# One encoder layer on one core: the last forgetting pair by squares and DRAM, two differential norms by squares

## The chip, the cores and the metric

The kernel runs on one core of a Trainium2 chip. The metric is the device time of one execution in microseconds. The core has a matrix engine (TensorE, "PE" in the profile, its weight loads "PEld"), three engines for elementwise work (VectorE "DVE", ScalarE "ACT", GpSimd "POOL"), and SyncE ("SP"), which here only issues transfers. Each engine works off its own list of instructions in the order in which they were built, and waits on semaphores for the others.

## The reference

The reference is one layer of a streaming encoder on 512 tokens of 1024 channels, all in float32. The first sub-layer has four token mixers that read one normed input, among them differential attention (4 heads, two score maps each) and forgetting attention (8 heads, frame-causal):

```python
# differential attention, per head
a = p[:, :, 0] - lam * p[:, :, 1]
ya = _rms_norm(a @ v, diff_norm) * (1.0 - lambda_init)     # norm over the head's 128 channels
# forgetting attention, per head (64 channels)
s = q @ k.T * scale + c_q[:, None] - c_k[None, :]          # c: cumulative sum of log-forget
yf = softmax(where(causal, s, -inf)) @ v
# merge
mixed = sum over n of sigmoid(h @ w_gate + b_gate)[n] * (branch[n] @ w_branch[n]), @ w_out
```

Cross-attention to 256 memory tokens and a gated MLP with a short convolution follow.

## The kernel before

**Arithmetic.** Every product is made of matmuls in a reduced float32 format on operands that are split into a high and a low part: `mm3` (L250) issues high by high, high by low and low by high. So each weight tile that comes from DRAM is cast by ScalarE (L198, "wh") and subtracted by VectorE (L199, "wl"), and each activation is split in the same way (`split`, L158).

**Jobs and background.** `run_blocks` (L212) takes jobs from a generator. A job is a weight tile of 128 x 1024 and a body of matmuls on it; weights are fetched three jobs ahead, into two raw tiles and four split ones. Beside the jobs there is a background (L47): the attention tasks are generators that yield a cost and a least distance to the next step, and are advanced between jobs. `bg.drain(name)` runs the named tasks to their end. The order in which the instructions of each engine then stand is set by the tile framework's scheduler, from its own timeline; `tc.issue_after` ties one instruction behind another.

**Order of the jobs** (`mixer_jobs`, L1202). After the convolution and the short convolution come the differential heads with the convolution branch's gates, then the values of the forgetting heads, then the projections of query and key of the four forgetting pairs, two heads each (`kv_blocks`), with jobs of the first branch's gates (`gate_blocks(0, "a")`, 12 jobs in all: two gates and a branch, four times) dealt out behind the pairs 1, 2 and 3 (L1238). Behind them the forgetting tasks are drained, and `last_branch_jobs` (L1347) begins the branch that reads the forgetting heads.

**A forgetting pair** (`f_task`, L1059). In each of the steps 0 to 3 one block of 128 queries is scored for both heads (`scores`), VectorE adds mask and bias and takes the row minimum (L1129), ScalarE takes the exponential (L1135), and both scale by the reciprocal (L1140, L1142). The probabilities lie with queries on partitions; the value products need keys there. For the pairs 0, 1 and 2 (`far`) VectorE transposes 32 x 32 squares (`turn_squares`, L854), SP stores the result to DRAM (`put`, L859) and loads it back with the squares in their places (`get`, L866), and `split_in_place` casts (L872) and subtracts (L873). For the pair 3 `to_keys_major` (L836) transposes blocks of 128 x 128 on TensorE (L247) into the PSUM bank "tr" and splits from there. The value products follow in two halves (`values`, L883) into two "av" banks, one a head, and are evacuated at the end (L1153, L1154), then split into `y["f"]`.

**A differential head** (`a_task`, L901). The heads 0 to 2 go the same way by DRAM, head 3 by TensorE. At the end each head is normed: four transposes on TensorE bring tokens onto partitions, ScalarE squares (L958), VectorE reduces (L960), GpSimd takes the power, VectorE scales (L962), and four transposes bring channels back, into a split (L970). The convolution's norm (`conv_norm_task`, L700) does without them: it transposes squares, reduces over 32 channels, and sums the four partial sums with one product by a tiled identity (`over_channels`, L877).

**Banks.** PSUM has eight banks: two each of "sc", "mm" and "av", one each of "tr0" and "tr1". Jobs take turns among tags (`bank()`, L97): "mm" and "tr0" from the heads on, "mm" alone from the last pair's step 2 on (`share_now("mm")`), "mm" and "av" again from the third job of the last branch on.

Of the kernel before, what the change touches and what calls it, by code (L numbers as in the profile page):

```python
# [25 lines left out]
P = 128  # L26
S = 512
D = 1024
NT = S // P
# [54 lines left out]
def hybrid_layer(ctx: ExitStack, tc: tile.TileContext, a: dict, out: bass.AP):  # L84
# [526 lines left out]
    def y8b():  # L611
        return m2bp.tile([P, 4, S], F32R, tag="y8b", name="y8b", bufs=2)
# [252 lines left out]
    def get(d, n, pt, local):  # L865
        SP.dma_start(part_of(pt[1], n, local).bitcast(F32), d.rearrange("(a j) (b x) -> (j b) a x", j=32, b=4))  # L866

    def split_in_place(n, pt, local):
        hi, lo = (part_of(x, n, local) for x in pt)
        raw = lo.bitcast(F32)  # L870
        with tc.issue_after(evacuations[0]):
            A.copy(hi, raw)  # L872
        V.tensor_tensor(lo, raw, hi.bitcast(F32), ALU.subtract)  # L873
# [6 lines left out]
    def by_token(x):  # L880
        return x.rearrange("p (t c) -> p t c", c=32)
# [13 lines left out]
    def pt_tiles():  # L895
        return tuple(m1p.tile([P, 2, 4, 4, 32], F32R, tag=n, name=n, bufs=2) for n in ("pth", "ptl"))
# [4 lines left out]
    def a_task(h, qk, v):  # L901
        es, pt, av = {}, None, None
        far = h < 3
        yield 0.0, 3.0
        for step in range(8 if far else 6):
            if step in ((5, 7) if far else (3, 5)):
                if av is None:
                    av = bank("av")
                vh, vl = (x[:, :, h * P:(h + 1) * P] for x in v[0])
                with tc.issue_after(steps_of[0]) if far else ExitStack():  # L910
                    values(av, lambda kt: ((vh[:, kt], 0), (vh[:, kt], 1), (vl[:, kt], 0)), pt,
                           step // 2 - (2 if far else 1))
            cost = 0.0
            if far:
                for qt in SPLITS.get(step, ()):
                    split_in_place(qt + 1, pt, qt % 2)
                    cost += 0.1 + 0.15 * qt
                for qt in GETS.get(step, ()):
                    if qt % 2 == 0:
                        pt = pt_tiles()  # L920
                    get(es.pop(qt)[:, 0], qt + 1, pt, qt % 2)
            elif 1 <= step <= 4:
                if step in (1, 3):
                    pt = pt_tiles()
                to_keys_major(es.pop(step - 1)[:, 0], step, pt, (step - 1) % 2)
                cost += 0.1 + 0.15 * step
            if step < 4:
                qt, w = step, (step + 1) * P
                e = es[qt] = e4()
                st = m1p.tile([P, 8], F32, tag="st8", name="st8", bufs=4)  # L930
                for c in range(2):
                    ps = bank("sc")
                    scores(ps, qk, c, qt * P, w)
                    V.tensor_tensor_reduce(e[:, c, :w], ps[:, :w], mask_a[:, S - w:], scale=-HD ** -0.5,
                                           scalar=3.0e38, op0=ALU.add, op1=ALU.min,
                                           accum_out=st[:, c:c + 1])
# [32 lines left out]
        if "a" not in y:  # L969
            y["a"] = (y8b(), y8b())  # L970
        split(ps2, y["a"][0][:, h], y["a"][1][:, h], half["dn"])
        yield 0.6, 0.0

# [84 lines left out]

    def f_task(p, qk, v):  # L1059
        f_steps[p] = 0  # L1060
        far = p < 3
        while f_steps[p - 1] < 4:
            yield 0.0, 0.5
        ck = []
# [7 lines left out]
        def turn_ready():  # L1072
            while ready:
# [2 lines left out]
                for j in range(2):  # L1076
                    turn_squares(turned[:, j, :w], e[:, j, :w])
                es[qt] = put(turned, w)
        for step in range(8 if far else 6):
            if step in ((5, 7) if far else (3, 5)):  # L1080
                if av is None:
                    av = [bank("av"), bank("av")]
                with tc.issue_after(steps_of[0]) if far else ExitStack():
                    for j in range(2):
                        hl = v[0][:, :, 2 * p + j]
                        values(av[j], lambda kt: ((hl[:, kt], 0), (hl[:, kt], 1)), pts[j],
                               step // 2 - (2 if far else 1))
            while step == (3 if far else 2) and f_steps[p - 1] < 8:
                yield 0.0, 0.5
            f_steps[p] = step + 1  # L1090
            cost = 0.0
            if step == 4:
                turn_ready()
            if far:
                for qt in SPLITS.get(step, ()):
                    for j in range(2):
                        split_in_place(qt + 1, pts[j], qt % 2)
                    cost += 0.1 + 0.3 * qt
                for qt in GETS.get(step, ()):
                    if qt % 2 == 0:  # L1100
                        pts = [pt_tiles() for _ in range(2)]
                    d = es.pop(qt)
                    for j in range(2):
                        get(d[:, j], qt + 1, pts[j], qt % 2)
            else:
                if step == 2:
                    share_now("mm")
                for qt in {2: (0, 1), 3: (2,), 4: (3,)}.get(step, ()):
                    if qt % 2 == 0:
                        pts = [pt_tiles() for _ in range(2)]  # L1110
                    e = es.pop(qt)
                    for j in range(2):
                        to_keys_major(e[:, j], qt + 1, pts[j], qt % 2)
                    cost += 0.4 + 0.3 * qt
            if step < 4:
                qt, w = step, (step + 1) * P
                e = es[qt] = e4()
# [26 lines left out]
                if far:  # L1144
# [57 lines left out]
    def mixer_jobs():  # L1202
# [695 lines left out]
```

## Time and profile before

| | before |
|---|---|
| median of 3 runs | 1047.57 us (1047.52 to 1048.46) |
| profiled execution | 1047.26 us |
| its span, first to last instruction | 1045.5 us |
| TensorE busy | 1035.8 us |
| VectorE busy | 809.6 us |
| ScalarE busy | 510.6 us |
| GpSimd busy | 143.3 us |

The time of an execution is a little longer than its span, which runs from the first to the last instruction. Busy times of TensorE overlap, because matmuls are pipelined: a matmul of 512 columns is listed with some 0.38 us, while the next one starts 0.23 us after it. The rows of the timeline begin with start and duration in us, then engine, line, operation, output<-input, shape and count; what stands in brackets is the idle time of the engine ahead of it and what ended that. In the groups the numbers behind the bar are the busy time in us and the mean of one in ns, then the idle time ahead. In the waits a row has the waiting instruction, whom it waited for, the total in us, how often, and the longest. In the table of stretches each engine's busy time stands with its count of instructions.

### The profile page before, as it was taken

To read this page: it belongs to the slowest core of one execution; us is meant where nothing else is said; L and a number is where in the kernel's file an instruction comes from. 1 tells how busy PE (TensorE), PEld (TensorE's weight loads), DVE (VectorE), ACT (ScalarE), POOL (GpSimd) and SP (SyncE) were. 2 spreads that over 40 slices of the span, in tenths; PEclk is the share of its full clock that TensorE was granted. 3 is DMA by queue.
4 is the path that set the end of the run, shared out by engine and by line. 5 is a ranking of instruction groups with operands and counts; after the bars stand their busy time and mean duration, and the time that the engine had idled before them with its cause. 6 is when DMAs were issued, how large, how long until landed. Compare 5 with 4: busy or idle time off the path is not lost.

```text
span 1045.5 us, 14417 instructions
## 1 busy us (share of the span) xinstructions
PE 1035.8 (99%) x5235; PEld 880.7 (84%) x5235; DVE 809.6 (77%) x1241; ACT 510.6 (49%) x838; POOL 143.3 (14%) x239
## 2 busy tenths in 40 slices
PE   9999999999999999999999999999999999999997
PEld 8888888888888988888888899998888888888886
DVE  7999998677787367878577898777767777667786
ACT  5322222376565365666444566555343333445662
POOL 4001000100010123342101031121112111111001
PEclk9999999999999999999999999999999999999999
DMA  8954333334433246666338744135676676626662
GB/s 271 311 156 100 101 101 101 91 91 121 142 104 109 62 122 178 184 165 158 120 124 287 237 134 127 62 108 184 193 240 229 214 227 217 220 82 183 216 214 82
DMA packets 187453, 166.48 MB, mean 159 GB/s; under 512 B 20415, under 2 KB 159148, under 8 KB 187381
## 3 DMA queue, kind: packets, MB, share of 16 engines
q1 hardware_dynamic: 178339, 133.80, 43.1%
q10 hardware_dynamic: 6482, 23.21, 6.1%
q0 software_dynamic: 2560, 8.54, 2.7%
q8 instruction: 41, 0.67, 0.3%
q14 instruction: 31, 0.25, 0.1%
HBM read 140.74 MB, written 24.79 MB: 158 GB/s over the span
## 4 chain that ended last, share of the span: by engine, by line
PE 99%; DMA 0%; DVE 0%; issue 0%; POOL 0%; POOLq 0%; DVEq 0%; SPq 0%; ACT 0%; ACTq 0%
PE ps_mm L241 47%; PE ps_av L241 30%; PE ps_tr L241 11%; PE ps_sc L241 7%; PE ps_tr L247 2%; PE ps_mm L459 1%; PE ps_av L459 1%; DMA xs<-in_x 0%; PE ps_tr L443 0%; DVE o L1788 0%; PE ps_av L443 0%; DVE nt L438 0%; DVE ge L1183 0%; DVE nt L412 0%; POOL st_m L285 0%
## 5 line engine op out<-in xcount | busy, mean ns | idle before, releaser
L198 ACT CAST wh<-wr 128x1024 fp32r<-128x1024 f32 (+1 forms) x140 | 146.5, 1047 | 233.5 <-PE ps_mm L241 121.2
L199 DVE TENSOR_TENSOR wl<-wr,wh 128x1024 fp32r<-128x1024 f32 (+1 forms) x140 | 174.8, 1249 | 86.2 <-ACT wh L198 85.4
L241 PE MATMUL ps_mm<-hth,wh 128*128 128x512 f32 (+1 forms) x536 | 198.9, 378 | 0.0
L241 PE MATMUL ps_mm<-htl,wh 128*128 128x512 f32 (+1 forms) x536 | 198.3, 377 | 0.0
L241 PE MATMUL ps_mm<-hth,wl 128*128 128x512 f32 (+1 forms) x536 | 198.3, 377 | 0.0
L241 PE MATMUL ps_av<-hth,wh 128*128 128x512 f32 (+1 forms) x328 | 122.5, 374 | 0.0
L241 PE MATMUL ps_av<-htl,wh 128*128 128x512 f32 (+1 forms) x328 | 122.5, 373 | 0.0
L241 PE MATMUL ps_av<-hth,wl 128*128 128x512 f32 (+1 forms) x328 | 122.3, 373 | 0.0
L241 PEld LDWEIGHTS ps_mm<-hth,wl 128*128 128x128 f32 x536 | 99.0, 188 | 18.3
L241 PEld LDWEIGHTS ps_mm<-hth,wh 128*128 128x128 f32 x536 | 99.0, 188 | 17.9 <-ACT hth L161 0.3
L241 PEld LDWEIGHTS ps_mm<-htl,wh 128*128 128x128 f32 x536 | 98.9, 188 | 17.9
L694 DVE SCALAR_TENSOR_TENSOR y<-y,par,y 128x508 f32<-128x508 f32 (+29 forms) x120 | 82.5, 725 | 0.1
L241 PEld LDWEIGHTS ps_av<-hth,wh 128*128 128x128 f32 x328 | 61.6, 188 | 11.1 <-DVE e L1154 0.3
L241 PEld LDWEIGHTS ps_av<-htl,wh 128*128 128x128 f32 x328 | 61.6, 188 | 10.9
L241 PEld LDWEIGHTS ps_av<-hth,wl 128*128 128x128 f32 x328 | 61.6, 188 | 10.9
L1689 DVE TENSOR_TENSOR wl<-dw,wh 128x1024 fp32r<-128x1024 f32 x32 | 40.2, 1260 | 15.0 <-ACT wh L1688 14.7
L1688 ACT CAST wh<-dw 128x1024 fp32r<-128x1024 f32 x32 | 33.4, 1051 | 22.2 <-PE ps_mm L241 7.4
L1636 ACT ACTIVATE th<-c 128x512 f32<-128x512 f32 x22 | 13.9, 632 | 48.8 <-DVE c L621 48.8
L1123 POOL TENSOR_SCALAR fbias<-ck,cq 128x128 f32<-128x128 f32 (+3 forms) x32 | 23.4, 739 | 73.0 <-DVE st L1129 66.6
L621 DVE SCALAR_TENSOR_TENSOR c<-ps_mm,par,c 128x510 f32<-128x510 f32 (+1 forms) x44 | 32.7, 744 | 0.7
L241 PE MATMUL ps_tr<-hth,wh 128*128 128x512 f32 x80 | 31.8, 398 | 0.0
L241 PE MATMUL ps_tr<-htl,wh 128*128 128x512 f32 x80 | 31.6, 395 | 0.0
(503 smaller groups left out, 2227.9 us busy)
## 6 DMA issues: line engine op xcount, KB each, us to landing
wr<-in_w_up SPq DMA_DIRECT2D x44, 512.0 KB
wr<-in_w_in SPq DMA_DIRECT2D x38, 512.0 KB
wr<-in_w_gate SPq DMA_DIRECT2D x32, 512.0 KB
wp<-in_w_down ACTq DMA_DIRECT2D x22, 512.0 KB
sums<-wp ACTq DMA_DIRECT2D x22, 512.0 KB
dw<-sums SPq DMA_DIRECT2D x44, 256.0 KB
wr<-in_w_branch SPq DMA_DIRECT2D x16, 512.0 KB
wide<-in_w_out SPq DMA_DIRECT2D x12, 512.0 KB
```

The costliest lines, as they stand in the source:

```text
L198: last_weights[:] = [order(A.copy(hi, raw[:, :n])).ins, low.tensor_tensor(lo, raw[:, :n], hi.bitcast(F32), ALU.subtract).ins]
L199: low.tensor_tensor(lo, raw[:, :n], hi.bitcast(F32), ALU.subtract).ins]
L241: steps_of[:] = [PE.matmul(ps, lhs, rhs, start=start, stop=stop).ins]
L247: turns.append(PE.transpose(ps, x, ident[:n, :n]).ins)
L459: keep(PE.matmul(banks[c][:, :S // 2], w[p == 1][:, k, c * P:(c + 1) * P], ht[p == 2][:, i * 4 + k, :S // 2], start=(i, p, k) == (0, 0, 0) ...
L621: ins = V.scalar_tensor_tensor(dst[:, s:], src[:, :S - s], w(k), dst[:, s:], ALU.mult, ALU.add)
L694: ins = V.scalar_tensor_tensor(dst[:, s:], src[:, :S - s], pc("conv_dw", k * 4 + j), dst[:, s:], ALU.mult, ALU.add)
L1123: G.tensor_scalar(bias[:, :w], ck[j][:, :w], -1.0, cq[:, qt, head:head + 1], ALU.mult, ALU.add)
L1636: A.activation(th, c[:, 0], AF.Silu)
L1688: A.copy(hi, x)
L1689: V.tensor_tensor(lo, x, hi.bitcast(F32), ALU.subtract)
```

## The change

1. `f_task`: all four pairs take the way by squares and DRAM. The condition `far`, the branch with `to_keys_major` and the call `share_now("mm")` go; pair 3 has eight steps like the others, and the scheduling costs are the same for all.
2. `a_task`: the heads 0 and 1 are normed by squares. VectorE transposes squares, ScalarE squares the values, VectorE reduces over 32 channels, one product by the tiled identity sums over the four groups of channels, GpSimd takes the power, VectorE scales and transposes back, and the split reads SBUF. The heads 2 and 3 keep the transposes of TensorE. The tile of the sums, "ms4", is wider and has one buffer where it had two.
3. The 12 jobs of the first branch are dealt out 2, 3 and 7 behind the pairs 1, 2 and 3, not 3, 3 and 6.

```diff
@@ a_task
+        if "a" not in y:
+            y["a"] = (y8b(), y8b())
+        if h < 2:
+            V.transpose(e[:, 1], e[:, 0])
+            A.activation(e[:, 0], e[:, 1], AF.Square, scale=1.0 / math.sqrt(P))
+            ms = m1p.tile([P, S // 32], F32, tag="ms4", name="ms4")
+            V.tensor_reduce(ms, by_token(e[:, 0]), AX.X, ALU.add)
+            yield 2.0, 4.0
+            ps = bank("tr")
+            over_channels(ps[:, :S // 32], ms)
+            V.tensor_scalar(ms, ps[:, :S // 32], EPS, None, ALU.add)
+            G.tensor_tensor(ms, ms, nhalf[:, :1].to_broadcast([P, S // 32]), ALU.pow)
+            yield 0.2, 4.0
+            V.tensor_tensor(by_token(e[:, 1]), by_token(e[:, 1]), ms.unsqueeze(2).to_broadcast([P, S // 32, 32]),
+                            ALU.mult)
+            V.transpose(e[:, 0], e[:, 1])
+            split(e[:, 0], y["a"][0][:, h], y["a"][1][:, h], half["dn"])
+            yield 2.4, 0.0
+            return
         ps = bank("tr")
...
-        ms = m1p.tile([P, NT], F32, tag="ms4", name="ms4", bufs=2)
+        ms = m1p.tile([P, S // 32], F32, tag="ms4", name="ms4")[:, :NT]
...
@@ f_task
-        far = p < 3
...
-        for step in range(8 if far else 6):
-            if step in ((5, 7) if far else (3, 5)):
+        for step in range(8):
+            if step in (5, 7):
...
-            while step == (3 if far else 2) and f_steps[p - 1] < 8:
+            while step == 3 and f_steps[p - 1] < 8:
...
-            else:
-                if step == 2:
-                    share_now("mm")
-                for qt in {2: (0, 1), 3: (2,), 4: (3,)}.get(step, ()):
-                    if qt % 2 == 0:
-                        pts = [pt_tiles() for _ in range(2)]
-                    e = es.pop(qt)
-                    for j in range(2):
-                        to_keys_major(e[:, j], qt + 1, pts[j], qt % 2)
-                    cost += 0.4 + 0.3 * qt
...
-                cost += 0.6 + 0.0038 * w
-                if far:
-                    ready.append((qt, e, w))
-                    cost += 0.003 * w
-            yield cost, 6.5 if far and step == 5 else 4.5
+                ready.append((qt, e, w))
+                cost += 0.6 + 0.0068 * w
+            yield cost, 6.5 if step == 5 else 4.5
@@ mixer_jobs
-            for _ in range((3, 3, 6)[p - 1]):
+            for _ in range((2, 3, 7)[p - 1]):
```

More of the change, by code (lines that the diff above doesn't have):

```diff
@@ L968, in a_task @@
             transpose(ps2[:, t * P:(t + 1) * P], e[:, 0, t * P:(t + 1) * P])
-        if "a" not in y:
-            y["a"] = (y8b(), y8b())
         split(ps2, y["a"][0][:, h], y["a"][1][:, h], half["dn"])
@@ L1078, in turn_ready @@
                 es[qt] = put(turned, w)
-        for step in range(8 if far else 6):
-            if step in ((5, 7) if far else (3, 5)):
+        for step in range(8):
+            if step in (5, 7):
                 if av is None:
                     av = [bank("av"), bank("av")]
-                with tc.issue_after(steps_of[0]) if far else ExitStack():
+                with tc.issue_after(steps_of[0]):
                     for j in range(2):
@@ L1086, in f_task @@
                         values(av[j], lambda kt: ((hl[:, kt], 0), (hl[:, kt], 1)), pts[j],
-                               step // 2 - (2 if far else 1))
-            while step == (3 if far else 2) and f_steps[p - 1] < 8:
+                               step // 2 - 2)
+            while step == 3 and f_steps[p - 1] < 8:
                 yield 0.0, 0.5
@@ L1093, in f_task @@
                 turn_ready()
-            if far:
-                for qt in SPLITS.get(step, ()):
-                    for j in range(2):
-                        split_in_place(qt + 1, pts[j], qt % 2)
-                    cost += 0.1 + 0.3 * qt
-                for qt in GETS.get(step, ()):
-                    if qt % 2 == 0:
-                        pts = [pt_tiles() for _ in range(2)]
-                    d = es.pop(qt)
-                    for j in range(2):
-                        get(d[:, j], qt + 1, pts[j], qt % 2)
-            else:
-                if step == 2:
-                    share_now("mm")
-                for qt in {2: (0, 1), 3: (2,), 4: (3,)}.get(step, ()):
-                    if qt % 2 == 0:
-                        pts = [pt_tiles() for _ in range(2)]
-                    e = es.pop(qt)
-                    for j in range(2):
-                        to_keys_major(e[:, j], qt + 1, pts[j], qt % 2)
-                    cost += 0.4 + 0.3 * qt
+            for qt in SPLITS.get(step, ()):
+                for j in range(2):
+                    split_in_place(qt + 1, pts[j], qt % 2)
+                cost += 0.1 + 0.3 * qt
+            for qt in GETS.get(step, ()):
+                if qt % 2 == 0:
+                    pts = [pt_tiles() for _ in range(2)]
+                d = es.pop(qt)
+                for j in range(2):
+                    get(d[:, j], qt + 1, pts[j], qt % 2)
             if step < 4:
@@ L1142, in f_task @@
                         A.activation(e[:, j, :w], e[:, j, :w], AF.Copy, scale=st[:, 6 + j:7 + j])
-                cost += 0.6 + 0.0038 * w
-                if far:
-                    ready.append((qt, e, w))
-                    cost += 0.003 * w
-            yield cost, 6.5 if far and step == 5 else 4.5
+                ready.append((qt, e, w))
+                cost += 0.6 + 0.0068 * w
+            yield cost, 6.5 if step == 5 else 4.5
         if "f" not in y:
```

## The prediction

> **What bounds the kernel now.** I read the page first: busy shares, the granted clock by slice, the chain that ended last; then TensorE's own waits, and last the timeline around the two places that the change touches.
>
> ```profile
> PE 1035.8 (99%) x5235; PEld 880.7 (84%) x5235; DVE 809.6 (77%) x1241; ACT 510.6 (49%) x838; POOL 143.3 (14%) x239
> PEclk9999999999999999999999999999999999999999
> PE 99%; DMA 0%; DVE 0%; issue 0%; POOL 0%; POOLq 0%; DVEq 0%; SPq 0%; ACT 0%; ACTq 0%
> ...
> L198 ACT CAST wh<-wr 128x1024 fp32r<-128x1024 f32 (+1 forms) x140 | 146.5, 1047 | 233.5 <-PE ps_mm L241 121.2
> L199 DVE TENSOR_TENSOR wl<-wr,wh 128x1024 fp32r<-128x1024 f32 (+1 forms) x140 | 174.8, 1249 | 86.2 <-ACT wh L198 85.4
> ```
>
> TensorE is busy for 1035.8 of 1045.5 us, at an undivided clock in every slice, and the chain that sets the end is TensorE for 99%. What TensorE waits for is in the view of waits, for that engine alone:
>
> ```profile
> PE ps_mm L400 <- DVE e L350: 1.3, 1, 1.3
> PE ps_tr L443 <- DVE nt L438: 1.2, 1, 1.2
> ```
>
> These two lie in the first ten microseconds; after them TensorE waits for nothing. So an instruction that TensorE no longer issues is worth its slot in full, and a wait of TensorE that is new costs its length in full. Work added on VectorE, ScalarE, SP or the DMA queues costs nothing by itself, only through such a wait.
>
> **What is saved.** A transpose goes down as 0.27 us of busy time, but they overlap, so I price them by starts, in the timeline of TensorE: four of the first head's norm, then groups of two and of three of the last pair.
>
> ```profile
> 284.24 0.39 PE L241 MATMUL ps_mm<-hth,wl 128*128 128x512 f32 x1
> 284.47 0.60 PE L247 MATMUL ps_tr<-ident,e 128*128 128x128 f32 x4
> 284.83 0.48 PE L241 MATMUL ps_mm<-hth,wh 128*128 128x512 f32 x1
> 285.14 0.40 PE L241 MATMUL ps_mm<-htl,wh 128*128 128x512 f32 x1
> ...
> 500.07 0.38 PE L247 MATMUL ps_tr<-ident,e 128*128 128x128 f32 x2
> 500.21 0.48 PE L241 MATMUL ps_mm<-hth,wh 128*128 128x512 f32 x1
> 500.53 0.40 PE L241 MATMUL ps_mm<-htl,wh 128*128 128x512 f32 x1
> ...
> 506.43 0.52 PE L247 MATMUL ps_tr<-ident,e 128*128 128x128 f32 x3
> 506.70 0.48 PE L241 MATMUL ps_mm<-hth,wh 128*128 128x512 f32 x1
> 507.01 0.40 PE L241 MATMUL ps_mm<-htl,wh 128*128 128x512 f32 x1
> ```
>
> From 284.47 to the next matmul's start at 284.83 are 0.36 us, and that matmul takes 0.31 to the one behind it where the usual step is 0.23: together 0.44 us for four. In the same way two cost 0.14 + 0.09 = 0.23, and three 0.27 + 0.08 = 0.35. The two norms lose four groups of four, 1.76 us. The last pair loses two groups of four, two of three, two of two and two single ones, which I take as a third group of two: 0.88 + 0.70 + 0.46 + 0.23 = 2.27 us. Together 4.03.
>
> Each norm gets one product with the tiled identity instead. The convolution's norm already has that product (it is recorded as two):
>
> ```profile
> 186.15 0.29 PE L877 MATMUL ps_tr<-bn,across 128*128 128x16 f32 x2
> 186.29 0.48 PE L241 MATMUL ps_mm<-y8b,wh 128*128 128x512 f32 x1
> 186.60 0.39 PE L241 MATMUL ps_mm<-y8b,wl 128*128 128x512 f32 x1
> ```
>
> From 186.15 to 186.60 are 0.45 us, less the 0.23 of the matmul between: 0.22 each, 0.44 for both. Saved on TensorE: 4.03 - 0.44 = 3.6 us.
>
> **What the other engines get.** Each norm gets two passes of squares (1.05 each by the row of 512 columns below) and a small sum more on VectorE. Its result is read only by the first branch's products, which need all four heads. Its own product with the identity could hold TensorE up; in the built order of the changed kernel 32 and 40 matmuls of 0.23 us, 7 and 9 us, stand between the head's last value product and that one, for a copy, a pass of squares, a Square and a reduction, some 3 us at 0.6 to 1.1 each. Nothing of this is on the path; with that cover gone it would be these 3 us, twice. The last pair's squares are new for VectorE:
>
> ```profile
> 419.99 0.72 DVE L854 STREAM_TRANSPOSE e<-e 128x128 f32<-128x128 f32 x2
> 427.81 1.18 DVE L854 STREAM_TRANSPOSE e<-e 128x256 f32<-128x256 f32 x2
> 433.91 1.63 DVE L854 STREAM_TRANSPOSE e<-e 128x384 f32<-128x384 f32 x2
> 438.43 2.10 DVE L854 STREAM_TRANSPOSE e<-e 128x512 f32<-128x512 f32 x2
> ```
>
> Two heads at each of the four widths: 0.72 + 1.18 + 1.63 + 2.10 = 5.6 us. The splits are as many as before, now from SBUF. The stage into which they fall has room for them:
>
> ```profile
> 460.00:505.00 45.00, 45.00 (x226) 38.05 (x225) 34.82 (x76) 26.86 (x59) 14.79 (x24) 1.00 0.59 161
> ```
>
> 34.8 of 45 us become 40.4, nine tenths. Four stores and eight loads are added on SP's queue; a weight load behind them is needed only four blocks of 5.4 us later, so 4 us of delay is covered. The deal of jobs adds no work: one job moves from between the first pairs to behind the last.
>
> **What the change puts on the path.** The last pair now goes the way of the first three: scores, softmax, squares, store to DRAM, load, split, value products. For the first three pairs other jobs cover that way. Here I counted the built order of the changed kernel. Behind the last pair's last score product TensorE has 72 matmuls of 512 columns (the rest of one gate block, a whole one, nine of the last branch's first output, a third gate block), the first half of the values, and then the second half. Nothing can stand ahead of that second half: the next output and the next gate need the two "av" banks, which the last pair's values hold, and both "mm" banks are taken. 72 x 0.228 is 16.4 us; with the first half and the first head's second half (0.9 each, from 517.70 to 518.58 below) and the switches (0.4), the second head's second half comes up 18.6 us behind that score product.
>
> When are its operands ready? Rows of the pairs with the second index 1 and 2:
>
> ```profile
> 430.59 0.63 PE L241 MATMUL ps_sc<-qk 128*128 128x512 f32 x2
> 440.55 0.36 SPq L859 DMA_DIRECT2D turned<-e  x1
> ...
> 466.88 1.08 PE L241 MATMUL ps_sc<-qk 128*128 128x512 f32 x4
> 481.98 0.37 SPq L859 DMA_DIRECT2D turned<-e  x1
> 486.27 0.91 SPq L866 DMA_DIRECT2D ptl<-turned  x2
> 490.79 0.62 ACT L872 CAST pth<-ptl 128x512 fp32r<-128x512 f32 x1 [1.71 <-DMA ptl<-turned]
> 491.44 0.69 DVE L873 TENSOR_TENSOR ptl<-ptl,pth 128x512 fp32r<-128x512 f32 x1 [1.28 <-ACT pth L872]
> 492.71 0.69 DVE L873 TENSOR_TENSOR ptl<-ptl,pth 128x512 fp32r<-128x512 f32 x1
> 494.71 0.45 PE L241 MATMUL ps_av<-ptl,v 128*128 128x128 f32 x2
> ```
>
> From the end of the last score product to the store: 440.55 - 431.2 = 9.4 us for one, 481.98 - 467.96 = 14.0 for the other. In the built order little stands between on VectorE: squares of 384 (1.63), four small splits (some 1.4), the scale (0.5), the pair before's two sums (1.4), squares of 512 (2.1), with 1.2 of waiting where ScalarE's exponentials stand behind a cast that awaits a load, and 1.8 ahead of it: 9.8 us, close to the quicker pair. The store is seen as landed 4.3 us after its issue (481.98 to 486.27). SP then has a load, a weight load and two more loads, 1.3 us by the steps of 0.4 shown. From the issue of such a load to the end of its second split are 492.13 - 486.27 = 5.9 us. 9.8 + 4.3 + 1.3 + 5.9 = 21.3, against 18.6: a wait of 2.7. The planner has so far set such products a little late (here the last split ended at 493.40 and the product that reads it began behind 494.6), so part of my sum may be too long; I take 2.2. The ends are 0, if that lead holds throughout, and 2.7 + 4.2 = 6.9, with the 14.0 of the slower pair.
>
> A second wait follows. Behind the values stands the next output, which takes the bank that the first head's values hold, until they are evacuated:
>
> ```profile
> 517.16 0.58 ACT L1153 COPY e<-ps_av 64x512 f32<-64x512 f32 x1 [1.47 <-PE ps_av L241]
> 517.70 0.28 PE L241 MATMUL ps_av<-pth,v 128*128 128x256 f32 x1
> 517.77 0.68 DVE L1154 TENSOR_TENSOR e<-ps_av,e 64x512 f32<-64x512 f32 x1 [1.36 <-ACT e L1153]
> 518.58 0.69 PE L241 MATMUL ps_av<-y,wh 128*128 128x512 f32 x2
> ```
>
> Before, three matmuls stood between the heads, and the bank came free at 518.45, just when TensorE reached 518.58. In the changed order a weight cast (1.05) stands ahead of the copy on ScalarE and a weight subtraction (1.25) ahead of the sum on VectorE, both behind the last splits. From the end of the last split: 0.4 for the cast's rest, 1.25, 0.68 = 2.3 us, of which the second head's own products cover 0.65: a wait of 1.7 (from 0, if that weight comes too late to be in the way, to 2.3).
>
> The last pair's second copy and sum and the split behind them, four steps of 0.6 to 0.7, then have 24 matmuls, 5.4 us, to hide behind: nothing is added.
>
> Sum against the profiled execution of 1047.26: - 3.6 + 2.2 + 1.7 = + 0.3, 1047.6. The median of the runs, 1047.57, stands 0.3 above it: forecast 1047.9 us, no change that a measurement can tell. I take 0.2%, 2.1 us, as the bound of that.
>
> **Rivals.** First, the squares come in time and the bank too: then 1047.57 - 3.6 = 1044.0. For it speaks that at all twelve such places of the first three pairs and heads TensorE did not wait; and loads can be quicker, as one of 128 KB shows:
>
> ```profile
> 274.27 0.37 SPq L866 DMA_DIRECT2D ptl<-turned  x1
> 276.62 0.41 ACT L872 CAST pth<-ptl 128x256 fp32r<-128x256 f32 x1 [1.62 <-DMA ptl<-turned]
> ```
>
> 2.35 us from issue to cast where I took 4.5. With waits of under 1.5 us in all the kernel is faster by more than the bound. Against it: those twelve places had matmuls to spare, this one has not. [...]
>
> Second, slower: the store is as late as in the slower pair. Then 6.9 + 1.7 - 3.6 = + 5.0, 1052.6. It decides from waits of 5.7 us on, that is from a store some 11.6 us behind the last score product, not 9.8. For it: two of ScalarE's exponentials stand behind casts that await loads, as they did in that pair (ACT L872 at 490.79 had waited 1.71 us). Against it: fewer weight splits stand between. [...]
>
> Third, VectorE becomes the bound between 460 and 505 us, nine tenths busy: the weight splits come late, and the 4.6 us that it has to spare are gone in waits for others. I price it at up to half the squares, 2.8, with the forecast's waits: 1050.7. Against it: the weights are split blocks ahead.
>
> **How the numbers follow.** Waits under 1.5 us: 0.26. The forecast, waits from 1.5 to 5.7: 0.48. A later store: 0.18. VectorE: 0.08. So faster 0.26, same 0.48, slower 0.26. The range goes from the first rival's 1044.0, below which I leave 0.08, to 1051.0, above which I leave 0.1.
>
> **What would show it.** TensorE with 34 transposes and products fewer. Right: in TensorE's waits two new rows near 510 us, value products waiting for a split and an output waiting for the "av" bank's evacuation, about 4 us together. A view of waits with nothing new means the first rival. The forecast is wrong if the store's distance from the last score product is not near 9.8, if its landing and the load's are not near 4.3 and 4.5, or if TensorE waits at other places.

## The result, and the profile after

| | before | after |
|---|---|---|
| median | 1047.55 us (1047.38 to 1048.46, 4 runs) | 1053.72 us (1052.48 to 1054.44, 4 runs) |
| profiled execution, its span | 1047.26, 1045.5 us | 1054.44, 1052.7 us |
| TensorE busy | 1035.8 us | 1035.2 us |

The changed kernel is slower: ratio 1.0058, 95% interval 1.0045 to 1.0070, that is 6.2 us. The forecast was 1047.9 us, with 1051.0 as its upper end; the nearest of the prediction's cases is its second rival, 1052.6.

TensorE's waits, after. The first two rows of before (L400, L443) are still there; these are new:

```profile
PE ps_av L241 <- DVE ptl L873: 3.2, 3, 2.5
PE ps_av L241 <- ACT pth L872: 1.9, 2, 1.6
...
PE ps_av L241 <- DVE e L1157: 1.0, 1, 1.0
PE ps_av L241 <- ACT pth L161: 0.7, 1, 0.7
PE ps_av L241 <- ACT e L952: 0.7, 1, 0.7
PE ps_tr L247 <- DVE ptl L162: 0.3, 1, 0.3
```

Nearly 8 us of waits. They lie at two places. In the table of stretches (busy time of PE, PEld, DVE, ACT and POOL with their counts, then the granted clock, the DMA share and GB/s) these are the two, first before, then after:

```profile
340.00:352.00 12.00, 11.96 (x101) 11.76 (x100) 3.69 (x8) 2.60 (x6) 1.72 (x3) 1.00 0.18 46
505.00:530.00 25.00, 24.90 (x128) 20.53 (x127) 11.07 (x15) 10.63 (x17) 0.99 (x2) 1.00 0.21 64
```

```profile
340.00:352.00 12.00, 10.31 (x83) 9.68 (x82) 5.64 (x17) 5.79 (x13) 2.76 (x5) 1.00 0.00 1
505.00:530.00 25.00, 18.85 (x82) 14.63 (x81) 10.96 (x14) 8.48 (x14) 0.00 (x0) 0.93 0.51 135
```

Between 340 and 352 us TensorE was idle for 0.04 us and now is for 1.69; between 505 and 530 for 0.10, and now for 6.15, at a mean clock of 0.93. After, in the timeline around the last pair:

```profile
496.70 1.15 PE L241 MATMUL ps_sc<-qk 128*128 128x512 f32 x4
...
500.40 9.94 SPq L859 DMA_DIRECT2D turned<-e  x2
507.88 2.08 DVE L854 STREAM_TRANSPOSE e<-e 128x512 f32<-128x512 f32 x2 [3.02 <-DMA turned<-e]
509.99 0.36 SPq L859 DMA_DIRECT2D turned<-e  x1
...
511.46 0.39 PE L241 MATMUL ps_av<-ptl,v 128*128 128x256 f32 x1 [2.51 <-DVE ptl L873]
511.58 1.88 SPq L866 DMA_DIRECT2D ptl<-turned  x2
513.55 0.79 SPq L182 DMA_DIRECT2D wr<-in_w_gate  x1
514.43 2.40 SPq L866 DMA_DIRECT2D ptl<-turned  x2
...
520.61 0.51 ACT L872 CAST pth<-ptl 128x384 fp32r<-128x384 f32 x1 [2.10 <-DMA ptl<-turned]
521.92 0.69 DVE L873 TENSOR_TENSOR ptl<-ptl,pth 128x512 fp32r<-128x512 f32 x1 [0.22 <-ACT pth L872]
521.95 0.39 PE L241 MATMUL ps_av<-pth,v 128*128 128x256 f32 x1 [1.62 <-ACT pth L872]
...
524.75 1.22 PE L241 MATMUL ps_av<-y,wh 128*128 128x512 f32 x2 [1.03 <-DVE e L1157]
528.04 0.40 PE L241 MATMUL ps_av<-y,wl 128*128 128x512 f32 x1
```

From top to bottom: the last score products (their rows end near 497.9); the third quarter's store, issued at 500.40 (its row is joined with that of the last store, which stands again at 509.99); the squares of the last quarter, which VectorE begins only at 507.88, after waiting 3.02 us for a DMA that reads the buffer "e"; the last store at 509.99; a value product of the first half, which waited 2.51 us for a split that stood behind those squares and a weight's subtraction on VectorE; the loads; a cast of the second head's third quarter, which waited 2.10 us for its load; the second head's second half, 1.62 us late; and the last branch's first output in an "av" bank, 1.03 us late.

The clock also fell. Two stretches of 3.6 us, one behind the other, after:

```profile
520.60:524.20 3.60, 1.43 (x8) 1.09 (x8) 2.58 (x4) 3.11 (x5) 0.00 (x0) 1.00 0.00 1
524.40:528.00 3.60, 3.25 (x8) 2.63 (x9) 1.67 (x3) 0.62 (x1) 0.00 (x0) 0.55 0.49 146
```

TensorE was busy for 1.43 of 3.6 us, and for the next 3.6 us the granted clock was 0.55. From 524.75 to the start at 528.04 are 3.29 us for eight matmuls, instead of 8 x 0.227 = 1.82: 1.47 us lost.

To see whether something is missing I summed, for every stage, by how much the starts of TensorE's instructions lie further apart than their columns take (0.227 us for 512 columns, 0.07 for a transpose):

| stage | before | after |
|---|---|---|
| 340 to 352 us | 1.2 | 3.6 |
| 505 to 530 us | 1.8 | 9.9 |
| all others, from 10 us on | 19.0 | 17.8 |

That is 8.1 + 2.4 - 1.2 = 9.3 us more, less 36 x 0.07 = 2.5 us of transposes: some 7 us, and the spans differ by 7.2. Outside the two stages the kernels agree within some 1.2 us.

### The profile page after: what moved, and what is told of

Same layout as the page of the kernel before. It is cut to its first block, busy times and chain, and to the rows that moved or that the text cites. A ratio compares the mean times of both kernels' runs of the same rounds, so it can differ in the third digit from the quotient of the medians.

```text
span 1052.7 us, 14391 instructions
## 1 busy us (share of the span) xinstructions
PE 1035.2 (98%) x5203; PEld 879.0 (83%) x5203; DVE 816.5 (78%) x1255; ACT 510.7 (49%) x838; POOL 145.4 (14%) x237
## 4 chain that ended last, share of the span: by engine, by line
PE 95%; DMA 2%; DVE 1%; issue 0%; SPq 0%; ACT 0%; POOL 0%; POOLq 0%; DVEq 0%; ACTq 0%
PE ps_mm L241 45%; PE ps_av L241 30%; PE ps_tr L241 11%; PE ps_sc L241 7%; PE ps_tr L247 2%; DMA turned<-e 1%; PE ps_mm L459 1%; PE ps_av L459 1%; DMA ptl<-turned 1%; DMA xs<-in_x 0%; DVE e L854 0%; DVE wl L199 0%; SPq L866 0%; DVE o L1791 0%; POOL st_r L419 0%
## 5 line engine op out<-in xcount | busy, mean ns | idle before, releaser
L198 ACT CAST wh<-wr 128x1024 fp32r<-128x1024 f32 (+1 forms) x140 | 146.6, 1047 | 241.9 <-PE ps_mm L241 134.4
L241 PE MATMUL ps_mm<-htl,wh 128*128 128x512 f32 (+1 forms) x528 | 195.2, 377 | 0.0
L241 PE MATMUL ps_mm<-hth,wh 128*128 128x512 f32 (+1 forms) x528 | 195.1, 377 | 0.0
L241 PE MATMUL ps_mm<-hth,wl 128*128 128x512 f32 (+1 forms) x528 | 194.9, 377 | 0.0
L241 PE MATMUL ps_tr<-hth,wh 128*128 128x512 f32 x88 | 34.8, 395 | 0.0
L241 PE MATMUL ps_tr<-htl,wh 128*128 128x512 f32 x88 | 34.7, 395 | 0.0
L241 PE MATMUL ps_tr<-hth,wl 128*128 128x512 f32 x88 | 34.5, 392 | 0.0
L854 DVE STREAM_TRANSPOSE e<-e 128x128 f32<-128x128 f32 (+3 forms) x44 | 31.4, 742 | 3.7 <-DMA turned<-e 3.4
```

The source lines that it names most:

```text
L198: last_weights[:] = [order(A.copy(hi, raw[:, :n])).ins, low.tensor_tensor(lo, raw[:, :n], hi.bitcast(F32), ALU.subtract).ins]
L241: steps_of[:] = [PE.matmul(ps, lhs, rhs, start=start, stop=stop).ins]
L854: V.transpose(dst, src.rearrange("p (t j b) -> p b t j", b=4, j=32))
```

## The experiments

All of them compute the whole layer. Ratios are to the kernel before, run beside them.

**The two parts apart.** First the norms alone, then the last pair and the deal alone:

```diff
@@ norms: before, and
+        if h < 2:
+            V.transpose(e[:, 1], e[:, 0])
...
@@ pair: after, and
-        if h < 2:
-            V.transpose(e[:, 1], e[:, 0])
...
```

> The kernel before with only the norms of the first two differential heads by squares; the last pair and the deal of jobs as before. Sixteen transposes at 0.11 us are gone, 1.76 us. If the new idle time of TensorE at 340 to 352 us (2.5 us in the changed kernel) comes from these norms: 1047.5 - 1.8 + 2.5 = 1048.3 us, and rows of TensorE waiting for ScalarE's casts near 347 and 350 us. If it does not: 1045.8 us and no such rows.

> The changed kernel with the norms as before: only the last pair by squares and the deal two, three, seven. If the two edits act apart: 1053.7 + 1.8 - 2.5 = 1053.0 us, with the waits behind the last pair (some 10 us of idle and slow time between 505 and 530 us) unchanged and none at 340 to 352. If the norms' later work makes the last pair late, the waits shrink: 1049 to 1051 us.

Measured: norms 1047.96 us, ratio 1.0007 (0.9998 to 1.0016); pair 1054.20 us, ratio 1.0069 (1.0052 to 1.0086). So the norms by squares save nothing that can be measured: their 1.3 us are eaten where the profile of that kernel has the same rows as the changed one, at the same place, with the last pair untouched:

```profile
PE ps_av L241 <- ACT pth L161: 0.7, 1, 0.7
PE ps_av L241 <- ACT e L952: 0.7, 1, 0.7
PE ps_tr L247 <- DVE ptl L162: 0.3, 1, 0.3
```

The pair alone carries the loss. Its waits are of the kinds of the changed kernel (a first half by 1.93 us at 510.74, the second head's second half by 0.95 and 0.34 from 520.97 on, the bank by 1.04), and its two stages stand at 1.2 and 8.6 in the measure of the table above. Within these intervals the two parts act apart.

**Why the norms' saving is lost.** A deal with one more job behind the last head, then the same instructions with the old norm's cost told to the planner, then the first head alone (at the old cost, and with the pair of hyb237, below):

```diff
@@ norms_0237
-        for h, n in enumerate((0, 2, 4, 6)):
+        for h, n in enumerate((0, 2, 3, 7)):
@@ norms_cheap
-            yield 2.0, 4.0
+            yield 0.75, 2.0
...
-            yield 0.2, 4.0
+            yield 0.75, 1.5
...
-            yield 2.4, 0.0
+            yield 0.6, 0.0
@@ hyb_norm0
-        if h < 2:
+        if h < 1:
```

> Only the norms by squares, with the gate jobs between the differential heads dealt none, two, three, seven instead of none, two, four, six: one job of 5.4 us more behind the last head. If TensorE idles at 346 to 351 us because the longer norm tasks hold back the last head and its tail has too little work beside it: no such rows, 1045.7 us. If the idle time comes from the order on ScalarE and VectorE and not from too little cover: it stays, or moves between the first heads, 1047.5 to 1048.5 us.

> Only the norms by squares, the same instructions, but with the planner told the cost and the waits of the old norm (0.75, 0.75 and 0.6 of cost, 2.0 and 1.5 of wait) instead of 2.0, 0.2 and 2.4 with 4.0 and 4.0. If the idle time of TensorE at 346 to 351 us comes from the planner, which by the higher cost sets the last head's work some 6 us later: the last head's last score product is back near 333 us, no such idle time, 1045.5 us. If it comes from the work itself on VectorE and ScalarE: 1047 to 1048 us.

> The last pair by squares for three quarters, and the norm by squares for the first head alone (0.9 us of transposes). If the idle time and the low clock at 340 to 350 us come from the second norm's work beside the last heads: none of it, 1045.0 us. If the first norm's work alone brings it: 1046 us or more.

Measured: norms_0237 1057.98 us (ratio 1.0097, 1.0082 to 1.0112); norms_cheap 1047.31 (1.0005, 0.9996 to 1.0015); hyb_norm0 1047.96 (1.0002, 0.9993 to 1.0011). In the timelines the last two score products of the last head begin at 333.0 us before, 339.2 in norms, 334.1 in norms_cheap and 342.0 in norms_0237. So half of my theory held: the planner's cost does set that head later, and the cheaper cost takes it back. But the idle time did not go with it:

```profile
PE ps_tr L247 <- DVE ptl L162: 1.2, 1, 1.2
```

```profile
340.40:344.00 3.60, 2.14 (x17) 1.71 (x16) 2.05 (x5) 2.00 (x4) 0.51 (x1) 0.99 0.00 0
344.00:347.60 3.60, 3.60 (x20) 3.60 (x19) 0.59 (x1) 0.59 (x1) 0.00 (x0) 0.53 0.00 0
```

With the cheap cost TensorE waits for a split on VectorE instead (1.2 us, ahead of transposes of a head's output at 342.59 us), and in the profiled execution the clock drops to 0.53 for 3.6 us on top. One job more behind the last head made it worse: its last scores came later still, with one job less ahead of them, TensorE waited 3.7 us for the scaling in a later head's norm, and the clock stood at 0.50 for 6.8 us. And one norm alone, with the pair of hyb237, costs some 1.5 us against hyb237 by the ratios, whose intervals just overlap: the same wait of 1.2, and a new one of 1.2 us for a gate's product on VectorE at 571 us. What is shown: under each of the four plans TensorE idles at 340 to 352 us (1.8, 4.3, 1.5 and 1.5 us; 0.04 before), about as long as the norms save or longer. Which of their instructions does it is not settled.

**Why the last pair is late: buffer and loads.** Three attempts at two suspects. The last squares get a place of their own (the score operands' buffer that the pair before has left); the memory branch's two loads of 512 KB, which GpSimd issues at 498 to 499 us, are put off.

```diff
@@ own_buffer
-                turned = e4()
+                turned = e4() if p < 3 or qt < 3 else m1p.tile([P, 6, S], F32, tag="qk", name="turned", bufs=2)[:, :2]
@@ late_mem (own_late: both)
-        G.dma_start(ns.gain, a["norm_mem"][0].partition_broadcast(P))
...
+        yield 0.0, 20.0
+        G.dma_start(ns.gain, a["norm_mem"][0].partition_broadcast(P))
         for t in range(2):
```

> The changed kernel with the two 512 KB loads of the memory branch (its gain and its first half), which GpSimd issues at 498 to 499 us, put off by some 20 us of other work. If these loads slow the stores of the last pair (seen landed 7 us after issue instead of 4.3): the last squares start 3 us earlier, the wait of 2.5 for the split goes and the bank waits shrink, some 1050 us. If the store is slow for another reason, or the buffer matters whatever the loads do: 1053 to 1054 us.

> The changed kernel with the last squares of the last pair written to the scores' operand buffer that the pair before has left, so that they need not wait until the store before has been read out of its buffer. If that wait (3.0 us on VectorE) is what makes the chain late: the last store about 3 us earlier, the 2.5 us wait of the value product gone, the clock kept, 1049 to 1050 us. If the loads' own duration or the bank is what counts: 1052.5 to 1054 us.

> Both edits at once in the changed kernel: the last squares in a buffer of their own, and the memory branch's two 512 KB loads put off. With the buffer alone the last store left 5 us earlier, but the two loads then left beside the last pair's own loads. If these two together are the whole delay: the second half's operands are there when TensorE comes, waits of TensorE behind the last pair under 1.5 us together, 1047 to 1049 us. If the pair's loads are slow beside the weight loads in any case: waits of 3 us or more stay, 1051 to 1054 us.

Measured: late_mem 1053.46 us, own_buffer 1054.40, own_late 1054.43; none better than the changed kernel. But late_mem tells nothing of the loads: they left at 498.54 us, where they leave at 498.42 in the changed kernel. own_buffer did what it should, and the loss moved:

```profile
505.40 0.36 SPq L859 DMA_DIRECT2D turned<-turned  x1
508.20 0.91 SPq L866 DMA_DIRECT2D ptl<-turned  x2
508.81 0.58 POOL L1269 DMA_DIRECT2D g_mem<-in_norm_mem  x1 [12.42 <-DMA turned<-turned]
509.38 0.54 POOL L1303 DMA_DIRECT2D m_t<-in_mem  x1
509.21 0.46 SPq L182 DMA_DIRECT2D wr<-in_w_gate  x1
509.75 3.63 SPq L866 DMA_DIRECT2D ptl<-turned  x1
516.97 0.62 ACT L872 CAST pth<-ptl 128x512 fp32r<-128x512 f32 x1 [1.70 <-DMA ptl<-turned]
517.64 0.39 PE L241 MATMUL ps_av<-pth,v 128*128 128x256 f32 x1 [2.47 <-ACT pth L872]
```

The last store leaves at 505.40 instead of 509.99 and no first half waits. But the memory branch's loads now leave at 508.81, beside the pair's loads (by the first POOL row GpSimd waits 12.42 us for the store out of that buffer; own_late has the same wait, and its loads leave at 508.42): the third of these takes SP 3.63 us to issue, the cast of the first head's last quarter comes at 516.97, and the product waits 2.47 us. So buffer and loads had to be taken away together, and with a wait that holds the loads back in truth:

```diff
@@ late2 (own_late2: with the buffer)
+        A.copy(ns.gain[:, :1], y["f"][0][:, 3, :1].bitcast(F32))
         G.dma_start(ns.gain, a["norm_mem"][0].partition_broadcast(P))
@@ own_late3: own_late2 and
+            if t == 0:
+                A.copy(m_t[:, :1], ns.gain[:, :1])
             G.dma_start(m_t, mem_d[t * P:(t + 1) * P, :])
```

> The changed kernel with the memory branch's two loads made to wait for the last pair's end (a copy of one column from its result goes ahead of them), about 526 us instead of 498. If they slow the last pair's stores and with them the buffer: the store of the third quarter is seen landed 4 to 5 us after its issue instead of 7, the last squares start near 505 us, the wait of 2.5 us shrinks below 1, 1050 to 1052 us. If the store is slow by itself: squares near 507.9 as before, 1053 to 1054 us.

> The same with the last squares in a buffer of their own, as in the two kernels before it, where the two loads then left at 508 us, beside the pair's own. If buffer and these loads together are the delay: last store near 505 us, loads of the second half landed within 5 us, waits behind the last pair under 1.5 us together, clock 1.0 throughout, 1047 to 1049 us. If the pair's loads are slow beside the two weight loads alone: a wait of 2 us or more near 515 to 521 us, 1050 to 1053 us.

> The changed kernel with the last squares in a buffer of their own and both loads of the memory branch held back until the last pair is done (in the two kernels before it, one or both left beside the pair's loads all the same). If buffer and these 1 MB of loads are the whole delay: second half's operands there in time, waits behind the pair under 1.5 us together, 1047 to 1049 us. If the pair's 0.9 MB and the two weight loads' 1 MB are by themselves more than the DMA engines move in the time (some 7 us at the 260 GB/s seen): operands near 515 and 519 us, waits of 2 to 4 us, 1050 to 1052 us.

Measured: late2 1052.98 us (1.0059), own_late2 1052.74 (1.0051), own_late3 1051.32 (1.0036, 1.0024 to 1.0048). In the first two one load was set ahead of the held one and left all the same, at 495.93 and 508.80 us. In late2 the squares start at 505.34, 2.5 us earlier than after, and wait for no DMA:

```profile
499.99 7.82 SPq L859 DMA_DIRECT2D turned<-e  x2
505.34 2.09 DVE L854 STREAM_TRANSPOSE e<-e 128x512 f32<-128x512 f32 x2
```

So the loads do slow the store that holds the buffer: 7.0 to 7.8 us from its issue to the squares in after, pair and late_mem, 5.4 here, where one of them left 3.1 us earlier and the other 26 us later. The first half's wait falls from 2.51 to 0.39 us, but late2's ratio is that of the changed kernel: this wait alone moves no time that the medians show. In own_late3 both are out of the way:

```profile
505.38 0.36 SPq L859 DMA_DIRECT2D turned<-turned  x1
506.82 0.37 SPq L182 DMA_DIRECT2D wr<-in_w_gate  x1
508.11 0.91 SPq L866 DMA_DIRECT2D ptl<-turned  x2
509.12 0.94 SPq L182 DMA_DIRECT2D wr<-in_w_gate  x1
510.15 2.01 SPq L866 DMA_DIRECT2D ptl<-turned  x2
515.95 0.51 ACT L872 CAST pth<-ptl 128x384 fp32r<-128x384 f32 x1 [2.10 <-DMA ptl<-turned]
517.28 0.69 DVE L873 TENSOR_TENSOR ptl<-ptl,pth 128x512 fp32r<-128x512 f32 x1 [0.24 <-ACT pth L872]
517.31 0.39 PE L241 MATMUL ps_av<-pth,v 128*128 128x256 f32 x1 [1.32 <-ACT pth L872]
```

The store leaves at 505.38, the first head is in time, and what is left is the second head: its cast waits 2.10 us for the load, the product 1.32. From the store to the end of the last load's issue pass 6.8 us (505.38 to 510.15 + 2.01): 2.7 until the first load leaves, then 4.1 for four loads and a weight load, of which the last two loads take 2.0; then 5.8 us until the last split ends at 517.97. So buffer and loads are worth 2.3 us together by the ratios (1.0058 to 1.0036; the two intervals just overlap), and waits of the size of the second expectation stay. That the queue and the weight loads cause these is argued from the rows; no run takes the weight loads away. The rest against the kernel before are these waits (1.7 us), the bank's (1.0), the norms' (1.7), and in other executions the clock.

**Cover and bank.** The deal, and the banks:

```diff
@@ deal138
-            for _ in range((2, 3, 7)[p - 1]):
+            for _ in range((1, 3, 8)[p - 1]):
@@ banks
-        yield next(gf)
-        yield next(gf)
+        for _ in range(3):
+            yield next(gf)
         yield share("mm", "av")
```

own_late_banks is own_late3 with the banks, and pair_all the same without the norms by squares.

> The changed kernel with its jobs dealt one, three, eight: 5.4 us more work behind the last scores, 5.4 less between the first two pairs. If the loss is a chain longer than its cover: the waits behind the last pair shrink from 10 to 3 us or less, 1047 to 1049 us, unless the first pairs now wait. If the value products are set early whatever the cover is: waits as before, 1053 to 1054 us.

> The changed kernel with only the banks altered: the last branch's first three jobs keep off the two av banks, so that nine more products (2.0 us) stand ahead of the second half's values. If the terms of the loss add up: 1053.7 - 2.0 for the cover - 1 for the bank = 1050.5 to 1051.5 us. If they overlap, because the operands still come late by more than the new cover: 1052 to 1053.5 us. If the low clock goes too, as TensorE idles in shorter pieces: below 1050 us.

> The same, and the last branch's first three jobs without the av banks, so that the second output's first nine products stand ahead of the values and need no bank of theirs: 2 us more cover. If the wait for the av bank is a real term of the loss: no wait for the evacuation, 1 to 3 us below the kernel beside it. If the next gate block then waits for the same bank: the same time within 0.7 us.

> The last pair wholly by squares with all three remedies (buffer of its own, memory branch's loads held back, banks), the norms as before. The kernel with the norms stood at 1047.7. If the norms by squares cost 0.4 to 0.7 us net there as they do alone: 1047.0 to 1047.3 us, no gain over the kernel before, against 1045.9 for the pair with its last quarter on TensorE. If the remedies leave the whole saving of 2.3 us: 1045.0 us.

Measured: deal138 1053.89 us (1.0061); banks 1051.24 (1.0042, 1.0025 to 1.0058); own_late_banks 1047.72 (1.0007, 0.9998 to 1.0016); pair_all 1051.38 (1.0042, 1.0027 to 1.0057). The deal moves no time: the last score products still end at 497.7 us, so no more work stands behind them; in its profile the waits there are 1.9 us shorter than after (4.2 instead of 6.1), and the clock is low for twice as long (0.86 in the stage, not 0.93). The banks alone give 2.5 us by the medians and 1.7 by the ratios, whose intervals overlap; in the profile, of the fastest execution, the first half still waits 1.35 us, the second head's second half only 0.42, and nothing waits for the bank. With all three remedies the stage behind the last pair is nearly as before:

```profile
505.00:530.00 25.00, 23.96 (x117) 19.93 (x116) 12.84 (x18) 10.08 (x16) 1.12 (x2) 1.00 0.57 155
```

Of own_late3's 2.69 us of idle time 1.04 are left, all of it for the bank: the next gate's first product, at 520.50, now waits for the evacuation. The step from own_late3 to own_late_banks, 3.6 us, is more than this: in own_late3 the mean clock of single executions fell to 0.994 (1052.15 us) where the profiled one had 0.998 (1049.52). pair_all should then have been the best of these, and is not: its executions spread from 1048.86 us (clock 0.998) to 1055.53 (0.995). In its profiled one, 1050.16 us, TensorE waits 0.8 us for the second head's operands and 1.0 for the evacuation, and then 0.3, 1.3 and 0.4 us at 533, 573 and 1026 us, where it does not wait before; in the measure of the table these places lose 4.3 us more than before, two thirds of it behind 530 us. I expected 1047; that is a miss, and what makes it so uneven is not settled, except that four of its five slowest executions have the lowest clocks (0.994 and 0.995).

**A version that beats both.** If the chain behind the last store is the loss, the last quarter need not go that way. The pair by squares for three quarters, the last one by TensorE; then the same with the norms by squares at the cheap cost:

```diff
@@ hyb237: pair, and in f_task
             for qt in SPLITS.get(step, ()):
-                for j in range(2):
-                    split_in_place(qt + 1, pts[j], qt % 2)
+                if p < 3 or qt < 3:
+                    for j in range(2):
+                        split_in_place(qt + 1, pts[j], qt % 2)
...
-                    get(d[:, j], qt + 1, pts[j], qt % 2)
+                    if p < 3 or qt < 3:
+                        get(d[:, j], qt + 1, pts[j], qt % 2)
+                    else:
+                        to_keys_major(d[:, j], qt + 1, pts[j], qt % 2)
...
-                ready.append((qt, e, w))
+                if p < 3 or qt < 3:
+                    ready.append((qt, e, w))
```

combo is hyb237 with the norms of norms_cheap.

> The last pair by squares for its first three quarters, its last quarter turned by TensorE as before; norms as before, jobs dealt two, three, seven. Twelve transposes at 0.11 us less, 1.4 us. If the chain behind the last store is what loses the time: no wait for a split near 510 to 522 us, 1046 to 1046.5 us. If the third quarter's squares, store and loads are late as well: a wait of 1 to 3 us, 1047.5 to 1050 us.

> The last pair by squares for three quarters and by TensorE for the last one, jobs two, three, seven, and the norms by squares at the old planner's costs. If the two savings are apart: 1045.9 - 1.8 = 1044.1 us, TensorE without new waits. If the norms still bring their idle time: 1046 us.

Measured: hyb237 1045.92 us, ratio 0.9988 (0.9978 to 0.9997); combo 1045.46, 0.9987 (0.9978 to 0.9996). Both are below both kernels, by 1.2 and 1.6 us of median below the one before, some 0.1%. Waits and stretch of hyb237:

```profile
PE ps_av L241 <- ACT pth L872: 0.3, 1, 0.3
```

```profile
505.00:530.00 25.00, 24.72 (x123) 20.47 (x122) 13.74 (x20) 12.85 (x22) 1.51 (x2) 1.00 0.34 89
```

One wait of 0.3 us is left of nearly 8. The saving is that of twelve transposes, within its interval of 0.3 to 2.3 us. In combo the norms bring next to nothing, with the same wait of 1.2 and the same drop of the clock at 344 us as in norms_cheap.

## Why the prediction was wrong

**What is saved: right.** hyb237 with 12 transposes less and no new wait gained 1.2 us (0.3 to 2.3 by the interval) where 12 x 0.11 = 1.4 were expected.

**"Nothing of this is on the path" (the norms): failed.** I weighed the norm's own product with the identity against its cover, and that one was indeed covered. I left out the heads behind the normed ones: 1.7 us of waits at 340 to 352 us, where I had counted 0, so the whole saving of 1.3. That the norms hold the last head back is shown (339.2 us instead of 333.0); the waits stay without it (norms_cheap), so by which step the norms cause them is open.

**The wait for the last pair's squares: right place, mis-sized.** This is the term that made the forecast miss. I summed 21.3 us from the last score product to the second head's last split, against 18.6 of cover: 2.2 of waiting. The same piece measured from 497.9 to 522.61, 24.7 us, and the waits for splits and casts at the last pair add up to 3.2 + 1.9 = 5.1. By terms: 9.8 to the store (its listed parts add up to 10.0) were 12.1, since I took the squares to start when VectorE was free, and did not ask which buffer they write; it was still being read by the store before, for 7.5 us where I knew 4.3 for a store without the two 512 KB loads beside it. Without the 3.02 us for that buffer the store would have left 9.1 us behind the score product, by the rows. 4.3 for the store's landing and 1.3 for SP's steps, 5.6, were 6.8 from 509.99 to the end of the last load's issue at 514.43 + 2.40: the two last loads alone held SP for 2.40 us, at a mean DMA share of 1.06 between 512 and 518 us (0.21 over 505 to 530 us before). 5.9 from the issue to the end of the split were 5.8, here from the end of that issue. And the late squares did harm once more than I counted: the split of the first half stood behind them on VectorE, 2.51 us of the 5.1. The prediction's upper end, 6.9, would have held; I chose near the quicker pair's row, and the slower pair's 14.0 us was nearer to 12.1.

**The wait for the "av" bank: right in place and cause.** 1.7 predicted, 1.03 measured, behind a weight's cast and subtraction as forecast; with nine products ahead that need no "av" bank it is gone (banks).

**The clock: not counted.** The forecast held nothing for it; it cost 1.47 us. No single wait of TensorE between 512 and 530 us was longer than 1.62 us; TensorE was busy for 1.43 of the 3.6 us from 520.60 on, and the clock was 0.55 over the 3.6 us from 524.40 on.

Sum with the measured terms: - 3.6 + 5.1 + 1.0 + 1.7 + 1.5 = + 5.7, against 7.2 between the two profiled executions, from which these terms come (6.2 between the medians). The table of the stages has 1.2 us more in the two places than these waits and the clock; I take that for the restarts around each wait, which the waits do not list: after, a value product of 256 columns took 0.23 us to the next start behind a wait (511.46 to 511.69) and 0.12 elsewhere (519.63 to 519.75).

**The rivals.** "The store is as late as in the slower pair", 1052.6, is what came nearest, at 1053.7, though it put the lateness down to exponentials behind casts that await loads, not to a buffer. Squares in time: excluded by the waits. VectorE as the bound: between 352 and 505 us TensorE lost nothing (5.7 and 5.2 us in the measure of the table), so no; but at one place VectorE's order made a split late that had its data.

## What to carry to other kernels

When work moves off the busiest engine to a way through memory, write down for its last piece every buffer that the way needs and who still reads it, and every transfer of any queue that runs at that time; a row of a quieter place is no price for it. Move only the pieces that have other work behind them: three quarters of the last pair gained 1.2 us, and the fourth cost 8. And a saving on the busiest engine counts only when the work behind it keeps its place: the norms' 1.3 us went in waits at other heads.

## What the runs showed of the hardware

- **The clock fell without a full pause.** It fell after stretches of 3.6 us in which TensorE was busy for 1.43 (after, 0.40) and 2.14 (norms_cheap, 0.59). The share in such a stretch does not decide; own_late3 had one like it, and the clock stayed:

```profile
516.00:519.60 3.60, 1.42 (x8) 1.08 (x8) 2.62 (x4) 3.10 (x5) 0.00 (x0) 1.00 0.00 1
519.60:523.20 3.60, 3.10 (x14) 2.56 (x15) 1.82 (x3) 0.90 (x3) 0.57 (x1) 1.00 0.47 146
```

In after it stood at 0.50 for 3.41 us (524.26 to 527.67), in norms_0237 for 6.8; the mean over the profiled execution was 0.997 in after, 0.995 in norms_0237 and 0.993 in own_buffer. What separates the stretches behind which it fell from own_late3's is not shown. That the clock makes the kernels with such a place uneven (pair_all spread over 6.7 us, banks over 5.6, the kernel before over 1.0 to 1.8) is an inference: one execution of each was traced.
- **An issue took microseconds.** A load on SP's queue mostly took 0.36 to 0.50 us to issue in these traces; beside the memory branch's 1 MB of loads one took 3.63 (own_buffer).
- **A store landed later beside other transfers.** The third quarter's 384 KB store of the last pair, issued at 500.40, held its buffer until 507.88; with one of the two 512 KB loads gone from there and the other 3.1 us earlier (late2) the squares behind it started 5.4 us after it, at 505.34, without a wait.
